# Two-layer GLA / short-convolution trunk on one core: TensorE order pinned in the ConvFFN, seven-product pairs for seven of eight convolution column tiles, split accumulation of the first two output products

## The chip, the cores and the metric

One core of a Trainium2 chip (trn2). The metric is the device time of one execution, in microseconds (us). Lower is better. The times are from the chip's own clock, the views from its hardware profiler.

## The reference, cut to what matters

Input x is (1, 512, 1024) in float32: 512 positions, model width 1024. Two layers, each a token mixer and a feed-forward, both with a residual:

```
layer 0: x += gla_mixer(rmsnorm(x));        x += conv_ffn(rmsnorm(x))
layer 1: x += short_conv_mixer(rmsnorm(x)); x += conv_ffn(rmsnorm(x))
out = rmsnorm(x)

conv_ffn(h):          up = causal_dwconv(h @ w_up, conv_w)     # 1024 -> 2 x 2816, 3 taps over positions
                      a, u = halves of up;  (silu(a) * u) @ w_down
short_conv_mixer(h):  b, c, u = thirds of h @ w_in             # 1024 -> 3 x 1024
                      (b * causal_dwconv(c * u, conv_w)) @ w_out
```

`causal_dwconv` is a depthwise convolution of width 3 over the positions.

## The kernel before, in words

**Layout.** Activations are held transposed: eight tiles `x[0..7]` of 128 channels x 512 positions. Every large product is made on TensorE in three terms: each operand is split into a high and a low part (`xh`, `xl` for activations, `wh`, `wl` for weights), and a product is wh*xh + wh*xl + wl*xh (`mm3`, line 302). A product group `group` (line 309) of eight 128-row blocks is therefore 24 matmuls of 512 columns; one of the FFN's down products, over a block of 6 or 5 gated tiles, is 18 or 15 of them.

**Seven products in place of eight.** Two column tiles of a projection that share the input (the `a` and `u` tiles of one FFN column, or the `c` and `u` tiles of one convolution column) can be made as a pair: seven half-size products (a Strassen form) in place of the eight that two groups amount to. `seven_first` (line 663) makes the first four, 48 matmuls of 256 columns, into two PSUM banks `updc` and `upab`; `seven_last` (line 680) the other three, 36 matmuls. The combinations are subtractions and additions of 256 columns on VectorE and copies on ScalarE (lines 670 to 689). The inputs they need beside `xparts`, sums and differences of x tiles named `t14..` and `t15..`, are made once per stage by `seven_sums` (line 598), called from `settle` (line 615) as the residual tiles come in, and split at the end of `settle`.

**Weights.** The class `Weights` (line 81) streams all weights in the order in which they are used. `load` starts a DMA on SyncE's queue into one of six raw buffers (`wr`, up to 512 KB each). `split_next` (line 163) makes a unit's `wh` on ScalarE (line 130) and its `wl` in one of two ways: on VectorE (line 135), or for units marked `added` by a negation on ScalarE (line 132) and an accumulating DMA issued from GpSimd (line 133). A pair takes two raw blocks and gives four units, q0 to q3 (`forms`, line 137): q0 needs two VectorE additions of the raw blocks (lines 144 and 146), the first into a buffer `s`, and q1 two more (150, 151); the halves are then split on ScalarE and VectorE. `take` (line 194) hands out the next unit and splits the one three further on. `wh` and `wl` have four buffers each.

**What sets the order.** The order of each engine's instructions is fixed when the kernel is compiled. A scheduler goes through a simulated clock: what stands earlier in the source goes first, but an instruction that is not ready by that clock gives way to a later one that is. On the chip each engine then keeps to the order so found, whether or not the data came when the simulated clock said. `tc.issue_after(ins)` puts what its block traces on the engine of `ins` behind `ins` in that order.

**The FFN** (`ffn_blocks`, line 692) goes through the list of `ff_steps` (line 213): column pairs 0 to 3 are made as plain groups ("up", "ua", "ub"), 4 to 21 by "s1" (`seven_first`) and "s2" (`seven_last`, then the convolution `conv` and `gate`). After each block of columns (`BLOCKS`, line 29) its eight down products "dn" are put between the steps of the next block. The steps around the end of the first block are, in the source:

```
... s1 5, ua 3, s2 5, s1 6, ub 3, s2 6, dn 0.0, s1 7, dn 0.1, s2 7, dn 0.2, s1 8, ...
```

`gate` makes the gated tile `g<j>` and splits it; `g3` (column 3, whose second half comes from "ub 3") is in `SOON`, that is, its low part is made on VectorE and not by the DMA.

**The convolution** (lines 744 to 769) makes columns 0, 1 and 7 as three plain groups `scc`, `scu`, `scb` and columns 2 to 6 (`SC_SEVEN`, line 32) as a pair around the group `scb`. Each column then goes through the three taps (`conv3`, line 362) and two multiplications, and is split into `s<i>`. The eight output products `so` follow as plain groups, each followed by `settle`. For the GLA's output products `go` (lines 638 to 643) the first two groups are already made together: blocks 0 to 5 of both, then blocks 6 and 7 of both.

Of the kernel before, what the change touches and what calls it, by code (L numbers as in the profile page):

```python
# [18 lines left out]
KD = D // P  # L19
# [9 lines left out]
BLOCKS = ((0, 6), (6, 11), (11, 16), (16, 22))  # L29
HALVED = 4  # L30
SOON = (3, 10, 15, 20, 21)
SC_SEVEN = (2, 3, 4, 5, 6)


@with_exitstack
def trunk_kernel(ctx, tc, xT, w_qk, w_v, w_g, w_up_gate, b_gate, w_go, w_sc, w_so, w_up, w_dn,
                 smalls, ff_cw, out):
    nc = tc.nc
    V, S, G, PE = nc.vector, nc.scalar, nc.gpsimd, nc.tensor
# [9 lines left out]
    def ps(name):  # L49
        return psp.tile([P, T], F32, tag="ps", name=name)  # L50
# [30 lines left out]
    class Weights:  # L81
# [3 lines left out]
        def __init__(self):  # L85
            self.units, self.srcs, self.need, self.last = [], [], [], []
            self.raw, self.split, self.hold = {}, {}, {}
            self.paired, self.added = set(), set()

            self.anchors = ()  # L90
            self.nl = self.ns = self.ng = 0

        def add(self, src, added=False):
# [43 lines left out]
        def forms(self, n, q, h, l):  # L137


            ra, rb = self.raw[n], self.raw[n + 1]  # L140
            lo, hi = slice(0, T), slice(T, 2 * T)
            if q == 0:
                s3 = bt(f"b13{'hl'[n % 4 // 2]}", f"s{n}")
                V.tensor_add(s3, ra[:, lo], rb[:, lo])  # L144
                self.halve(h[:, lo], l[:, lo], s3)
                V.tensor_add(rb[:, lo], rb[:, lo], rb[:, hi])
                self.halve(h[:, hi], l[:, hi], rb[:, lo])
            elif q == 1:
                self.halve(h, l, ra)
                V.tensor_add(ra[:, lo], ra[:, lo], rb[:, lo])  # L150
                V.tensor_add(ra[:, hi], ra[:, hi], ra[:, lo])
            elif q == 2:
                self.halve(h, l, rb[:, hi])
            else:
                self.halve(h, l, ra)
# [38 lines left out]
        def take(self):  # L194

            for _ in range(2):
                if self.nl < len(self.srcs) and (self.nl < 6 or self.last[self.nl - 6] < self.ns):
                    self.load()
                    if self.nl not in self.paired:
                        break  # L200
            self.part()
            self.ng += 1
            return self.split.pop(self.ng - 1)
# [9 lines left out]
    def ff_steps():  # L213
        steps = [("up", 0), ("up", 1), ("ua", 2), ("s1", 4), ("ub", 2), ("s2", 4), ("s1", 5), ("ua", 3), ("s2", 5)]

        middle = [("ub", 3)]
        for b in range(1, len(BLOCKS)):
            j0, j1 = BLOCKS[b]
            dn = [("dn", b - 1, m) for m in range(KD)]
            for j in range(j0, j1):  # L220
                steps += [("s1", j), middle.pop() if j == j0 else dn.pop(0), ("s2", j)]
                if j1 - j < len(dn) or j == j0 and b > 1:
                    steps.append(dn.pop(0))
            middle = dn
        return steps + middle + [("dn", len(BLOCKS) - 1, m) for m in range(KD)]
# [76 lines left out]
    def mm3(out, wparts, xparts, first, last, w_moving=False):  # L302
        (wh, wl), (xh, xl) = wparts, xparts
        terms = ((wh, xh), (wh, xl), (wl, xh)) if not w_moving else ((wh, xh), (wl, xh), (wh, xl))
        for i, (a, b) in enumerate(terms):
            a, b = (b, a) if w_moving else (a, b)
            PE.matmul(out, lhsT=a, rhs=b, start=first and i == 0, stop=last and i == 2)  # L307
# [325 lines left out]
    def residual(src, gi):  # L633
        for m in range(KD):
            settle(m, src(m), gi, True)


    go, w = [ps("go0"), ps("go1")], [take(), take()]
    for ks in (range(0, 6), range(6, 8)):
        for m in range(2):  # L640
            for k in ks:
                mm3(go[m], w[m][k], yparts[k], k == 0, k == KD - 1)
    residual(lambda m: go[m] if m < 2 else group(f"go{m}", yparts), 1)


    def product(out, ws, xs, first):
# [16 lines left out]
    def seven_first():  # L663

        dc, ab = ps("updc"), ps("upab")
        w1, w2 = halves(take())
        product(dc[:, lo], w1, tf[2], True)
        product(dc[:, hi], w2, tf[0], False)
        e = wk("e7", (P, HT), bufs=1)
        S.copy(e, dc[:, hi])  # L670
        V.tensor_sub(e, dc[:, lo], e)
        w1, w2 = halves(take())
        product(ab[:, lo], w1, cut(range(4), lo), True)
        product(ab[:, hi], w2, cut(range(4, 8), lo), False)
        u = wk("u", bufs=3)
        S.copy(u[:, lo], ab[:, hi])
        V.tensor_add(u[:, lo], u[:, lo], ab[:, lo])
        return dc, ab, e, u
# [11 lines left out]
        return u, u1  # L690

    def ffn_blocks(l, gnext):
        gp, cs, r = {}, {}, None

        def conv(j, i, u, src):
            V.tensor_mul(u, src, r)  # L696
            cs[j, i] = conv3(u, ffcw[:, l, i * NFF + j, :], f"c{i}", j == 0)

        def gate(j):
            a, u = cs.pop((j, 0)), cs.pop((j, 1))  # L700
            S.activation(a, a, AF.Silu)
            V.tensor_mul(u, u, a)
            gp[j] = split_to(u, f"g{j}", f"b{j % 11}", j not in SOON)

        for st in ff_steps():
            if st[0] == "dn":
                _, b, m = st
                last = b == len(BLOCKS) - 1
                if gnext is None and last and m == HALVED:
                    break  # L710
                part = group(f"dn{m}", [gp[j] for j in range(*BLOCKS[b])])
                if last and gnext is not None:
                    settle(m, part, gnext, False)
                else:
                    V.tensor_add(x[m], x[m], part)
                    if last:
                        norm_squares(m)
                continue
            step, j = st
            if step == "s1":  # L720
                begun = seven_first()
            elif step == "s2":
                for i, u in enumerate(seven_last(*begun)):
                    conv(j, i, u, u)
                gate(j)
            else:
                tiles = {"up": (0, 1), "ua": (0,), "ub": (1,)}[step]
                ups = {}
                for i in tiles:
                    ups[i] = group(f"up{i}", xparts)  # L730
                    if j == 0 and i == 0:
                        sums = sum_parts(acc[0])
                if j == 0:
                    r = inv_rms_rows(sums, D)
                for i in tiles:
                    conv(j, i, wk("u", bufs=3), ups[i])
                if 1 in tiles:
                    gate(j)
        return [gp[j] for j in range(*BLOCKS[-1])]

    ffn_blocks(0, 2)
# [3 lines left out]
    for i in range(KD):  # L745
# [20 lines left out]
        V.tensor_mul(cv, cv, r)  # L766
        V.tensor_mul(cv, cv, bp)
        yparts.append(split_to(cv, f"s{i}", f"b{i}", i < KD - 2))
    residual(lambda m: group(f"so{m}", yparts), 3)


    gp = ffn_blocks(1, None)
# [136 lines left out]
```

## Time and profile before

| | |
|---|---|
| median of 3 runs | 1097.52 us (1096.43 to 1100.97) |
| the profiled execution, its own time | 1096.32 us |
| its span, first to last instruction | 1094.6 us |
| mean granted TensorE clock | 0.994 of full speed |
| TensorE matmul busy | 1079.5 us (99%), 6502 matmuls |
| VectorE busy | 851.9 us (78%) |
| ScalarE busy | 684.2 us (63%) |
| DMA, mean over the span | 148 GB/s |

The profile is of one execution. Times in the views are microseconds from the start of the span. The FFN of layer 0 runs from about 211 to 561 us, the convolution from 561 to 689, its output products to 732.5, and the FFN of layer 1 from there to the end. PE is TensorE's matmuls, DVE VectorE, ACT ScalarE, POOL GpSimd, SP SyncE; L144 is line 144 of the kernel. In the timeline a bracket at the end of a row is the idle time of the engine ahead of the instruction and what ended it. Matmuls are pipelined: one row's duration overlaps the next, so the distance between starts is what counts.

### The profile page before, as it was taken

Reading aid. Unit: us, or ns where it says so; the run is one execution under the profiler, and the core shown is the slowest. Engines: PE = TensorE matmul, PEld = TensorE weight load, DVE = VectorE, ACT = ScalarE, POOL = GpSimd, SP = SyncE. Lnnn points to the kernel's source line nnn. Section 1 sums busy time; section 2 is a strip of 40 time slices with the busy share of each in tenths; the row PEclk is TensorE's granted clock in tenths of the full one; section 3 lists DMA queues with packets and bytes.
Section 4 is the critical chain, followed back from the end, with each engine's and each line's share of the span. In section 5 each row is a group of like instructions: output and inputs, shape, how many; then the busy total and the mean of one; then the engine's idle time right before and its main releaser. Section 6 shows DMA issues by size and latency. Waiting matters only on the chain.

```text
span 1094.6 us, 16998 instructions
## 1 busy us (share of the span) xinstructions
PE 1079.5 (99%) x6502; PEld 967.8 (88%) x6502; DVE 851.9 (78%) x1339; ACT 684.2 (63%) x1062; POOL 128.2 (12%) x160
## 2 busy tenths in 40 slices
PE   9999999999999999999999999999999999999997
PEld 7888888889899999999878998888989999999987
DVE  8874675789778989999678675477977888989954
ACT  7565765867656656666695455486755656666664
POOL 1000001101110111101111001011101011111120
PEclk9999999999999999999999999999999999999998
DMA  8332124865474564655897459386647556566573
GB/s 288 110 95 78 58 78 113 195 162 138 122 177 131 146 169 123 168 150 140 185 220 193 107 150 248 99 186 154 167 122 169 142 136 157 136 155 173 131 149 97
DMA packets 55958, 161.92 MB, mean 148 GB/s; under 512 B 6146, under 2 KB 8962, under 8 KB 55876
## 3 DMA queue, kind: packets, MB, share of 16 engines
q1 hardware_dynamic: 35428, 107.34, 31.1%
q0 software_dynamic: 20448, 53.49, 26.6%
q8 instruction: 51, 0.84, 0.3%
q14 instruction: 31, 0.25, 0.1%
HBM read 105.23 MB, written 2.10 MB: 98 GB/s over the span
## 4 chain that ended last, share of the span: by engine, by line
PE 68%; issue 3%; DMA 2%; DVE 1%; POOL 0%; ACT 0%; DVEq 0%; POOLq 0%; SPq 0%; ACTq 0%
PE updc L651 20%; PE dn L307 17%; PE upab L651 15%; PE scb L307 4%; PE so L307 4%; PE up L307 3%; PE dnl L307 2%; PE scu L307 1%; PE scc L307 1%; DMA wl<-wr 1%; DMA wr<-in_w_up 0%; POOL wl L133 0%; DVE wl L135 0%; DVE c L366 0%; DVE u L696 0%
## 5 line engine op out<-in xcount | busy, mean ns | idle before, releaser
L130 ACT CAST wh<-wr 128x1024 fp32r<-128x1024 f32 (+4 forms) x302 | 259.2, 863 | 187.3 <-PE upab L651 76.7
L135 DVE TENSOR_TENSOR wl<-wr,wh 128x512 fp32r<-128x512 f32 (+2 forms) x200 | 193.5, 981 | 60.0 <-ACT wh L130 59.2
L133 POOL DMA_DIRECT2D wl<-wr x102 | 89.2, 875 | 648.6 <-ACT wl L132 358.4
L365 ACT ACTIVATE c<-u,ffcw 128x512 f32<-128x512 f32 x88 | 59.3, 717 | 55.3 <-DVE u L696 55.3
L651 PE MATMUL upab<-xh,wh 128*128 128x256 f32 x328 | 92.8, 283 | 0.0
L651 PE MATMUL upab<-xl,wh 128*128 128x256 f32 x328 | 92.8, 283 | 0.0
L651 PE MATMUL upab<-xh,wl 128*128 128x256 f32 x328 | 92.8, 283 | 0.0
L132 ACT ACTIVATE wl<-wh 128x1024 fp32r<-128x1024 f32 (+2 forms) x102 | 90.8, 890 | 1.3
L366 DVE SCALAR_TENSOR_TENSOR c<-u,ffcw,c 128x511 f32<-128x511 f32 x88 | 62.4, 748 | 2.8 <-ACT c L365 2.6
L651 PEld LDWEIGHTS upab<-xh,wh 128*128 128x128 f32 x328 | 63.0, 192 | 0.0
L651 PEld LDWEIGHTS upab<-xl,wh 128*128 128x128 f32 x328 | 63.0, 192 | 0.0
L651 PEld LDWEIGHTS upab<-xh,wl 128*128 128x128 f32 x328 | 63.0, 192 | 0.0
L367 DVE SCALAR_TENSOR_TENSOR c<-u,ffcw,c 128x510 f32<-128x510 f32 x88 | 62.2, 746 | 0.0
L307 PE MATMUL up<-xh,wh 128*128 128x512 f32 x128 | 49.9, 390 | 0.0
L307 PE MATMUL up<-xl,wh 128*128 128x512 f32 x128 | 49.9, 390 | 0.0
L307 PE MATMUL up<-xh,wl 128*128 128x512 f32 x128 | 49.8, 389 | 0.0
L651 PE MATMUL updc<-xh,wh 128*128 128x256 f32 x164 | 46.4, 283 | 0.0
L651 PE MATMUL updc<-xl,wh 128*128 128x256 f32 x164 | 46.4, 283 | 0.0
L651 PE MATMUL updc<-xh,wl 128*128 128x256 f32 x164 | 46.4, 283 | 0.0
L696 DVE TENSOR_TENSOR u<-u,r 128x512 f32<-128x512 f32 x72 | 46.2, 684 | 0.0
L144 DVE TENSOR_TENSOR s<-wr,wr 128x512 f32<-128x512 f32 x41 | 28.2, 689 | 22.0 <-DMA wr<-in_w_up 15.3
L359 DVE RECIPROCAL r<-r 128x512 f32<-128x512 f32 x8 | 26.8, 3353 | 20.7 <-ACT r L358 20.7
(708 smaller groups left out, 3463.7 us busy)
## 6 DMA issues: line engine op xcount, KB each, us to landing
wr<-in_w_up SPq DMA_DIRECT2D x88, 512.0 KB, 3.9
wl<-wr POOLq DMA_DIRECT2D x38, 512.0 KB, 5.6
wr<-in_w_dn SPq DMA_DIRECT2D x32, 384.0 KB, 3.4
wl<-wr POOLq DMA_DIRECT2D x32, 384.0 KB, 4.1
wr<-in_w_sc SPq DMA_DIRECT2D x24, 512.0 KB, 4.4
wr<-in_w_dn SPq DMA_DIRECT2D x32, 320.0 KB, 3.2
wl<-wr POOLq DMA_DIRECT2D x32, 320.0 KB, 4.4
wr<-in_w_v SPq DMA_DIRECT2D x8, 512.0 KB, 3.7
```

What stands on the lines that cost most here:

```text
L130: S.copy(hh, src)
L132: S.activation(ll, hh.bitcast(F32), AF.Copy, scale=-1.0)
L133: G.dma_start(ll, src, accum_op=ALU.add)
L135: V.tensor_sub(ll, src, hh.bitcast(F32))
L144: V.tensor_add(s3, ra[:, lo], rb[:, lo])
L307: PE.matmul(out, lhsT=a, rhs=b, start=first and i == 0, stop=last and i == 2)
L359: V.reciprocal(r, r)
L365: a = S.activation(c, u, AF.Copy, scale=cw[:, 2:3])
L366: V.scalar_tensor_tensor(c[:, 1:], u[:, :T - 1], cw[:, 1:2], c[:, 1:], op0=ALU.mult, op1=ALU.add)
L367: v = V.scalar_tensor_tensor(c[:, 2:], u[:, :T - 2], cw[:, 0:1], c[:, 2:], op0=ALU.mult, op1=ALU.add)
L651: PE.matmul(out, lhsT=a, rhs=b, start=first and k == 0 and i == 0, stop=k == 3 and i == 2, skip_group_check=not first)
L696: V.tensor_mul(u, src, r)
```

## The change

Five edits. (1) `SC_SEVEN` is 1 to 7 in place of 2 to 6: convolution columns 1 and 7 are made as pairs as well. (2) The output products of the convolution are made as those of the GLA: the first two groups together, blocks 0 to 5 of both and then blocks 6 and 7 of both (`out_product`). (3) In the list of FFN steps the first down product of the first block moves behind the next "s1": `s2 6, s1 7, dn 0.0, s2 7, dn 0.1, s1 8, ...`; from column 10 on the list is as before. (4) In the FFN all TensorE instructions but those of the last eight down products are held to the order of the source (`manual_schedule`). (5) The two VectorE additions of a pair's unit q0 are queued behind the subtraction `e` (line 671) of the `seven_first` that was traced last, and the second of them moves ahead of the first split.

```diff
-SC_SEVEN = (2, 3, 4, 5, 6)
+SC_SEVEN = (1, 2, 3, 4, 5, 6, 7)
...
+            self.pace = None
...
             if q == 0:
                 s3 = bt(f"b13{'hl'[n % 4 // 2]}", f"s{n}")
-                V.tensor_add(s3, ra[:, lo], rb[:, lo])
+                with ExitStack() as behind:
+                    if self.pace is not None:
+                        behind.enter_context(tc.issue_after(self.pace))
+                    V.tensor_add(s3, ra[:, lo], rb[:, lo])
+                    V.tensor_add(rb[:, lo], rb[:, lo], rb[:, hi])
                 self.halve(h[:, lo], l[:, lo], s3)
-                V.tensor_add(rb[:, lo], rb[:, lo], rb[:, hi])
                 self.halve(h[:, hi], l[:, hi], rb[:, lo])
...
-                if j1 - j < len(dn) or j == j0 and b > 1:
+                if (j1 - j < len(dn) if j > j0 else b > 1):
                     steps.append(dn.pop(0))
...
-    go, w = [ps("go0"), ps("go1")], [take(), take()]
-    for ks in (range(0, 6), range(6, 8)):
-        for m in range(2):
-            for k in ks:
-                mm3(go[m], w[m][k], yparts[k], k == 0, k == KD - 1)
-    residual(lambda m: go[m] if m < 2 else group(f"go{m}", yparts), 1)
+    def out_product(name, gi):
+
+        o, w = [ps(f"{name}0"), ps(f"{name}1")], [take(), take()]
+        for ks in (range(0, 6), range(6, 8)):
+            for m in range(2):
+                for k in ks:
+                    mm3(o[m], w[m][k], yparts[k], k == 0, k == KD - 1)
+        residual(lambda m: o[m] if m < 2 else group(f"{name}{m}", yparts), gi)
+
+    out_product("go", 1)
...
-        V.tensor_sub(e, dc[:, lo], e)
+        W.pace = V.tensor_sub(e, dc[:, lo], e).ins
...
+        steps = ff_steps()
+        with tc.manual_schedule(engines={mybir.EngineType.PE}):
+            for st in steps[:-KD]:
+                take_step(st)
+        for st in steps[-KD:] if gnext is not None else steps[-KD:HALVED - KD]:
+            take_step(st)
         return [gp[j] for j in range(*BLOCKS[-1])]
...
-    residual(lambda m: group(f"so{m}", yparts), 3)
+    out_product("so", 3)
```

The body of the loop over the steps becomes the function `take_step`, otherwise unchanged.

## Rows read from the trace of the kernel before

**Rows 1.** The page's table of engines: busy time, share of the span, instructions.

```profile
PE 1079.5 (99%) x6502; PEld 967.8 (88%) x6502; DVE 851.9 (78%) x1339; ACT 684.2 (63%) x1062; POOL 128.2 (12%) x160
```

**Rows 2.** The table of waits: total us, times, longest; TensorE's largest entry.

```profile
PE dn L307 <- ACT g3h L130: 5.1, 2, 2.7
```

**Rows 3.** Timeline of TensorE, layer 0: start, duration, instruction, idle before.

```profile
284.92 0.40 PE L307 MATMUL dn<-g0h,wh 128*128 128x512 f32 x1
...
287.22 0.28 PE L651 MATMUL updc<-t150h,wl 128*128 128x256 f32 x1
290.21 0.70 PE L307 MATMUL dn<-g3h,wh 128*128 128x512 f32 x1 [2.71 <-ACT g3h L130]
...
299.33 0.40 PE L307 MATMUL dn<-g0h,wh 128*128 128x512 f32 x1
```

**Rows 4.** Timeline of TensorE, layer 1: the same two starts.

```profile
806.80 0.40 PE L307 MATMUL dn<-g0h,wh 128*128 128x512 f32 x1
...
821.10 0.40 PE L307 MATMUL dn<-g0h,wh 128*128 128x512 f32 x1
```

**Rows 5.** Chain of waits, an FFN stretch without idle time: start, length, work.

```profile
344.47 2.88 PE updc L651 x24
347.35 2.88 PE upab L651 x24
350.23 4.11 PE dn L307 x18
```

**Rows 6.** Busy time in windows; PEclk is the granted clock.

```profile
290.00:295.00 5.00, 4.79 (x18) 4.13 (x19) 5.00 (x10) 1.98 (x4) 0.00 (x0) 0.66 0.92 216
```

**Rows 7.** Timeline of VectorE, layer 0, ahead of that wait.

```profile
283.95 0.69 DVE L144 TENSOR_TENSOR s<-wr,wr 128x512 f32<-128x512 f32 x1 [4.24 <-issue]
284.56 0.68 DVE L696 TENSOR_TENSOR u<-up,r 128x512 f32<-128x512 f32 x1
...
290.68 0.69 DVE L135 TENSOR_TENSOR g3l<-c,g3h 128x512 fp32r<-128x512 f32 x1
```

**Rows 8.** Timeline of VectorE, layer 1, the same place.

```profile
805.52 0.69 DVE L144 TENSOR_TENSOR s<-wr,wr 128x512 f32<-128x512 f32 x1 [3.93 <-DMA wr<-in_w_up]
```

**Rows 9.** Chain of waits through the convolution and its output products.

```profile
578.82 5.44 PE scc L307 x24
...
595.14 2.87 PE updc L651 x24
...
610.67 2.88 PE updc L651 x24
...
626.21 2.88 PE updc L651 x24
...
689.18 43.52 PE so L307 x192
```

**Rows 10.** Timeline of TensorE and VectorE: end of column 6's pair, and its results.

```profile
672.55 0.28 PE L651 MATMUL upab<-t143h,wl 128*128 128x256 f32 x1
...
674.98 0.42 DVE L687 TENSOR_TENSOR u<-updc,u 128x256 f32<-128x256 f32 x1
...
683.62 0.69 DVE L135 TENSOR_TENSOR s6l<-c,s6h 128x512 fp32r<-128x512 f32 x1 [0.69 <-ACT s6h L130]
```

**Rows 11.** Busy time in windows: an FFN step, columns 6 and 7 (third value DVE).

```profile
423.43:436.93 13.50, 13.50 (x101) 12.89 (x100) 12.31 (x21) 8.45 (x14) 1.75 (x2) 1.00 0.43 121
...
657.13:672.67 15.54, 15.54 (x110) 14.58 (x109) 7.16 (x12) 9.98 (x13) 4.05 (x5) 1.00 1.04 249
672.67:689.02 16.35, 16.35 (x75) 13.53 (x73) 12.76 (x18) 5.36 (x7) 0.00 (x0) 1.00 0.65 206
```

**Rows 12.** Groups by line and shape: xcount | busy us, mean ns of one | idle before.

```profile
L135 DVE TENSOR_TENSOR wl<-wr,wh 128x1024 fp32r<-128x1024 f32 x112 | 136.7, 1222 | 56.4 <-ACT wh L130 56.1
```

**Rows 13.** Timeline of VectorE at the start of the convolution.

```profile
569.58 0.69 DVE L135 TENSOR_TENSOR t153l<-tl,t153h 128x512 fp32r<-128x512 f32 x1
...
575.83 3.35 DVE L359 RECIPROCAL r<-r 128x512 f32<-128x512 f32 x1 [4.87 <-ACT r L358]
```

**Rows 14.** Timeline of TensorE: the first group of the convolution.

```profile
562.20 0.50 PE L307 MATMUL scc<-xh,wl 128*128 128x512 f32 x1 [0.57 <-DMA wl<-wr]
```

More of the change, by code (lines that the diff above doesn't have):

```diff
@@ L692, in ffn_blocks @@
     def ffn_blocks(l, gnext):
-        gp, cs, r = {}, {}, None
+        gp, cs = {}, {}
+        r = sums = begun = None
         def conv(j, i, u, src):
@@ L703, in gate, with take_step @@
             gp[j] = split_to(u, f"g{j}", f"b{j % 11}", j not in SOON)
-        for st in ff_steps():
+        def take_step(st):
+            nonlocal r, sums, begun
             if st[0] == "dn":
@@ L708, in ffn_blocks @@
                 last = b == len(BLOCKS) - 1
-                if gnext is None and last and m == HALVED:
-                    break
                 part = group(f"dn{m}", [gp[j] for j in range(*BLOCKS[b])])
@@ L717, in ffn_blocks @@
                         norm_squares(m)
-                continue
+                return
             step, j = st
```

## The prediction

> **What bounds the kernel now.** I read the page's table of engines first: TensorE's matmuls are busy 99% of the span, every other engine 78% or less [rows 1]. Such a busy share alone does not say that TensorE works at its peak, so I then went down TensorE's timeline and looked at the distances between starts. From the output products of the GLA on they are those of a stream without holes: 43.52 us for 192 matmuls of 512 columns, 0.2267 us each [rows 9], and 2.88 us for 24 matmuls of 256 columns, 0.120 us each [rows 5]. The kernel is bound by TensorE's issue of matmuls. A change pays only where it takes matmuls out or closes a hole.
>
> The holes are few. In the table of waits TensorE's largest entry is one wait that occurs twice, 5.1 us in all: a down product waits for `g3h` [rows 2]. The timeline shows it in layer 0: dn 0.0 starts at 284.92 and goes through its first three blocks, three matmuls of "s1 7" follow, and then the array stands for 2.71 us until `g3h` is there [rows 3]. After it the granted clock is 0.66 in the mean over 290 to 295 us [rows 6]: part of that stretch ran at the lower of the two levels, 1.2 in place of 2.4 GHz, after TensorE had stood still. So the hole costs more than the wait. What it costs in all is read by comparing equal work: from the first matmul of dn 0.0 to that of dn 0.1 TensorE does one "dn" of 18 matmuls and one "s1" of 48. Without a hole these take 2.88 + 2.88 + 4.11 = 9.87 us [rows 5]. Here they took 299.33 - 284.92 = 14.41 [rows 3] in layer 0 and 821.10 - 806.80 = 14.30 [rows 4] in layer 1. **The loss is 4.54 and 4.43 us, 8.97 together.**
>
> Why `g3h` is late stands on VectorE. Its addition for the next pair's q0 (line 144) stands idle for 4.24 us before it starts [rows 7]; in layer 1 the same idle time, 3.93, is ended by the landing of a raw weight block [rows 8]. Behind that addition, in the same queue, sits the first operation on "ub 3", the multiplication `u<-up,r`, which starts at 284.56, the moment the addition is over; `g3l` ends 6.81 us after that, at 291.37 [rows 7]. The addition was put there by the compiler, whose simulated clock took the block to be landed.
>
> **The change part by part.** *The moved step (edit 3).* With "s1 7" ahead of dn 0.0, the product starts not at 284.92 but 5.76 us later, at 290.68, and asks for `g3h` after its first three blocks, 9 x 0.2267 = 2.04 us on, at 292.7. In the old trace `g3h` was there at 290.2 [rows 3] and `g3l` at 291.37 [rows 7]. So even if VectorE still stood for the raw block, both are there, by 1.3 us or more. What "s1 7" needs, its weights q0 and q1, sits ahead in the stream either way; q0 is now split one unit earlier in the source. Late next would be q1, which "s1 7" needs 2.88 us after its start.
>
> *The additions behind `e` (edit 5).* Unit q0 of a pair is split during the step before, after that step's `seven_first`. Its two additions now wait in VectorE's queue behind `e`, after that step's first 24 matmuls, 2.88 us [rows 5], and a copy on ScalarE, some 3.5 us in. Behind them on VectorE wait the split of q0 and whatever the scheduler puts later; TensorE waits for q0 at the next "s1". The tightest step is 13.50 us long with VectorE busy for 12.31 of it [rows 11], so about 10 us remain for two additions of 0.69 and two half splits of 0.69 [rows 7]. Cost on the path: nothing, covered by those 10 us; without that cover, each us late is a us of TensorE. The gain is that the multiplication on "ub 3" is no longer held up by the raw block, some 4 us more margin for `g3`. Edits 3 and 5 cure the same hole, so together they bring its 8.97 us once. Bounds: 0 (another operand is late at the new place) and 8.97. I take 8.97, since two margins stand behind it.
>
> *The fixed order (edit 4).* In the old trace the order on TensorE differs from that of the source only at these two places; everywhere else in both FFNs "s1", "dn" and "s2" come as listed. So it removes the three stray matmuls of rows 3 and moves nothing else: 0. It does take away the compiler's filling in.
>
> *Two more pairs (edit 1).* A column of three plain groups takes 595.14 - 578.82 = 16.32 us, one with a pair 626.21 - 610.67 = 15.54 [rows 9], so each pair saves 0.78, **1.56 for two**. The Trainium skill (TensorE: Matmul & The Clock Gate, Back-to-back issue gap) gives a warm gap of N/2.4 + 2.5 ns, that is 216 ns for 512 columns and 109 for 256; by it 48 x 216 - 84 x 109 would save 1.2 us per pair, 2.4 in all. The rows say 0.2267 and 0.120 us, and I go by the rows. What a pair adds elsewhere: on VectorE four additions and three half splits of 0.69 [rows 7], two whole splits of 1.22 [rows 12] and five operations of 0.42 [rows 10], 9.4 us; on GpSimd two accumulating DMAs fewer; on SyncE the same loads in the same order. For column 1 this starts in VectorE's idle 4.87 us ahead of the reciprocal, and the `t` tiles, which are now wanted at 578.8 and no longer at 595.1 [rows 9], are written by 570.3 [rows 13]. For column 7 VectorE has 7.16 + 12.76 us busy of the last 31.9 [rows 11]; with 9.4 more it is full but not over. I cost that at nothing on the path up to the output products.
>
> *The output products (edit 2).* They save no matmul. They are the cover for column 7, whose three taps now start only when its last product is done. From the end of column 6's pair (672.55 + 0.28) to the end of `s6l` (683.62 + 0.69) it was 11.5 us [rows 10], with about 2.4 us of weight splits in between (two of 1.22 [rows 12]), so 9.1 to 11.5 us. The cover is 36 matmuls (blocks 0 to 5 of two groups), 8.16 us, and block 6 of the first group, 0.68; the low part of `s7` is wanted one matmul later, at 9.07. The hole is 0 to 2.4 us. The scheduler may also pull block 6 of the second group ahead, 0.68. I take 0.7. The first two `settle` calls move together, later by 4 us for the first one only; the last one, which the next FFN waits for, stays.
>
> Sum: -8.97 - 1.56 + 0.7 = -9.8 us. On the profiled execution's 1096.32 that is 1086.5; the median of the runs shown, 1097.52, lies 1.2 above it and would give 1087.7. I say **1087.0**. Ends from the costs alone: without the hole of column 7 and without the 0.57 us that the first group waits [rows 14], 1084.5; with its full 2.4 us, 1088.2, on the upper base 1089.4.
>
> **The rivals.** *A: a new hole around the convolution's pairs.* Column 7's chain or the first pair's weights come 2 to 3 us late, and the clock falls as it did after the wait of 2.71 us, which cost 4.54. For it: VectorE is full there. Against: the five pairs of before flow without a hole, one every 15.54 us [rows 9]. It gives back about 4.5: 1087.0 + 4 = 1091.
>
> *B: the FFN's hole is only moved.* "s1 7" or dn 0.0 now waits for a split weight, which VectorE had behind the raw block. Half of the 8.97 stays: 1091.5. Against: q0 and q1 move earlier along with everything VectorE does.
>
> *C: slower.* The additions behind `e` make q0 late in every step, because VectorE is 91% busy [rows 11] and its order was laid out by a simulated clock; with the order fixed, TensorE cannot do a later product meanwhile. There are 17 such hand-overs per FFN, 34 in all (columns 5 to 21). The gain of 9.8 is gone at 0.29 us per step, and by 0.6 us each the time is 1097 + 20 - 10 = 1107. Against: the 10 us of room.
>
> *D: nothing.* The hole stays, because `g3` is as late by the new schedule as its consumer: 1096.
>
> **How the numbers follow.** The forecast has 0.62, A 0.14, B 0.10, D 0.06, C 0.08. The range 1084 to 1093 holds the forecast, and A and B but for their upper ends, about 0.83. A measurement here tells about 0.5%, 5.5 us, from no change: faster means under 1092.0, slower over 1103.0. Faster: 0.62, most of A and half or more of B, 0.77. Same: the rest of A and B, D and the milder part of C, 0.15. Slower 0.08.
>
> **What would show it.** Right: in the table of waits TensorE's wait for `g3h` is gone, from the start of dn 0.0 to the start of "s2 7" it takes 4.1 us, no window in either FFN has a granted clock under 1.00, and `s` (line 144) comes after `e` on VectorE. Columns 1 and 7 take 15.5 us each. At the first `so` groups a hole of under 1.5 us. Wrong: TensorE waiting for `wl` at "s1" all through the FFNs (C), for `s7` by 2 us with the clock down after it (A), or for anything around 285 to 293 us (B, D).

## The result, and the profile after

| | before | changed |
|---|---|---|
| median of 4 runs each | 1097.3 us (1096.43 to 1100.97) | 1086.14 us (1085.82 to 1086.49) |
| ratio, 95% interval | | 0.9892 (0.9869 to 0.9915) |
| profiled execution, its own time | 1096.32 us | 1086.49 us |
| its span, mean granted clock | 1094.6 us, 0.994 | 1084.8 us, 0.997 |

The changed kernel is 1.1% faster. The forecast was 1087.0, 0.9 above the median. The two profiled spans lie 1094.6 - 1084.8 = 9.8 us apart, the size of the forecast's sum.

Where the 9.8 us came from is read on TensorE's timeline: the starts of the first matmuls of each stage, subtracted from one another. For later use the table has the two kernels of the experiments that have the cleanest convolution with five and with seven pairs.

| stage of TensorE | before | changed | five pairs, no hole | seven pairs, no hole |
|---|---|---|---|---|
| start to the GLA's output products | 167.14 | 167.65 | 167.09 | 166.92 |
| first FFN, first `up` to first `scc` | 350.36 | 345.78 | 345.76 | 345.81 |
| convolution, to the first `so` | 128.00 | 126.24 | 127.14 | 125.55 |
| its output products, to the next `up` | 43.52 | 43.92 | 43.52 | 43.91 |
| second FFN, to the first `dnl` | 333.92 | 329.49 | 329.46 | 329.96 |

(five pairs: `e4_five_pairs`, seven: `g4_dve_splits`, both below.) The FFNs became 4.58 and 4.43 us shorter, 9.01 in all; the convolution 1.76; its output products 0.40 longer; the start 0.5 longer, which varies by as much from one execution to another (166.88 to 167.65 over all profiles here).

The page's table of engines, changed kernel; it answers to [rows 1]. There are 72 matmuls more and 4.7 us less of busy time.

```profile
PE 1074.8 (99%) x6574; PEld 967.2 (89%) x6574; DVE 871.6 (80%) x1367; ACT 684.4 (63%) x1070; POOL 124.4 (11%) x156
```

The table of waits, changed kernel, TensorE's four largest entries (total us, times, longest). The entry for `g3h` of [rows 2] is gone. What is largest now lies at the kernel's first and last matmuls; the fourth is the convolution's first group, as in [rows 14].

```profile
PE warm L76 <- DVE warm L64: 1.5, 1, 1.5
PE sums L811 <- DVE sq L802: 0.6, 1, 0.6
PE rb L824 <- DVE rl L818: 0.6, 1, 0.6
PE scc L313 <- DMA wl<-wr: 0.4, 1, 0.4
```

TensorE's timeline, changed kernel, at the place of [rows 3] and [rows 4] (start, duration, instruction). From the first matmul of dn 0.0 to the first of "s2 7" it takes 295.31 - 291.20 = 4.11 us in layer 0 and 811.24 - 807.14 = 4.10 in layer 1, the 4.11 of a `dn` without a hole in [rows 5].

```profile
291.20 0.40 PE L313 MATMUL dn<-g0h,wh 128*128 128x512 f32 x1
...
295.31 0.28 PE L660 MATMUL updc<-t150h,wh 128*128 128x256 f32 x1
...
807.14 0.40 PE L313 MATMUL dn<-g0h,wh 128*128 128x512 f32 x1
...
811.24 0.28 PE L660 MATMUL updc<-t150h,wh 128*128 128x256 f32 x1
```

Busy time in windows, changed kernel (the value after POOL's is the granted clock): the stretch of [rows 6], and column 7 as a pair. The first has a clock of 1.00 in place of 0.66, and TensorE busy throughout; so have all 138 windows of 5 us over the two FFNs, 211 to 556 us and 727 to 1072. In the second VectorE has 11.17 of 15.54 us.

```profile
290.00:295.00 5.00, 5.00 (x29) 4.35 (x28) 5.00 (x10) 2.77 (x7) 0.86 (x1) 1.00 0.75 213
...
667.65:683.19 15.54, 15.54 (x110) 14.58 (x109) 11.17 (x16) 6.14 (x9) 0.66 (x1) 1.00 0.75 208
```

VectorE's timeline, changed kernel, layer 0, at the place of [rows 7]. The multiplication `u<-up,r` starts at 281.98, where it was 284.56, and `g3l` at 287.75 in place of 290.68, though everything starts 0.5 us later here. The pair's addition `s` stands behind `e`, at 294.01, and has no idle time.

```profile
281.98 0.68 DVE L706 TENSOR_TENSOR u<-up,r 128x512 f32<-128x512 f32 x1
...
287.75 0.69 DVE L137 TENSOR_TENSOR g3l<-c,g3h 128x512 fp32r<-128x512 f32 x1
...
290.68 0.42 DVE L680 TENSOR_TENSOR e<-updc,e 128x256 f32<-128x256 f32 x1
...
294.01 0.68 DVE L149 TENSOR_TENSOR s<-wr,wr 128x512 f32<-128x512 f32 x1
```

The chain of waits, changed kernel, through the convolution, as in [rows 9]: column 1's `c` and `u` products begin at 574.58 and the next column's at 590.11, 15.53 us later; column 7's begin at 667.81 and the output products at 683.35, 15.54 later. The output products take 43.92 us to 727.27.

```profile
574.58 2.87 PE updc L660 x24
...
590.11 2.88 PE updc L660 x24
...
667.81 2.88 PE updc L660 x24
...
683.35 9.32 PE so L313 x41
...
727.27 10.88 PE up L313 x48
```

### The profile page after: what moved, and what is told of

Same layout as the page of the kernel before. It is cut to its first block, busy times and chain, and to the rows that moved or that the text cites. A ratio compares the mean times of both kernels' runs of the same rounds, so it can differ in the third digit from the quotient of the medians.

```text
span 1084.8 us, 17188 instructions
## 1 busy us (share of the span) xinstructions
PE 1074.8 (99%) x6574; PEld 967.2 (89%) x6574; DVE 871.6 (80%) x1367; ACT 684.4 (63%) x1070; POOL 124.4 (11%) x156
## 4 chain that ended last, share of the span: by engine, by line
PE 95%; issue 2%; DMA 1%; POOL 0%; DVE 0%; SPq 0%; ACT 0%; DVEq 0%; POOLq 0%
PE updc L660 23%; PE dn L313 17%; PE upab L660 17%; PE up L313 8%; PE so L313 4%; PE scb L313 4%; PE g L313 4%; PE v L313 4%; PE go L313 4%; PE k L313 2%; PE q L313 2%; PE dnl L313 2%; DMA wl<-wr 1%; PE o L536 1%; PE scu L313 1%
## 5 line engine op out<-in xcount | busy, mean ns | idle before, releaser
L137 DVE TENSOR_TENSOR wl<-wr,wh 128x1024 fp32r<-128x1024 f32 (+2 forms) x208 | 200.6, 980 | 56.5 <-ACT wh L132 56.0
L135 POOL DMA_DIRECT2D wl<-wr x98 | 84.8, 865 | 657.8 <-ACT wl L134 316.2
L660 PE MATMUL upab<-xl,wh 128*128 128x256 f32 x344 | 97.4, 283 | 0.0
L660 PE MATMUL upab<-xh,wl 128*128 128x256 f32 x344 | 97.4, 283 | 0.0
L660 PE MATMUL upab<-xh,wh 128*128 128x256 f32 x344 | 97.4, 283 | 0.0
L134 ACT ACTIVATE wl<-wh 128x1024 fp32r<-128x1024 f32 (+2 forms) x98 | 86.5, 883 | 1.4
L660 PEld LDWEIGHTS upab<-xh,wl 128*128 128x128 f32 x344 | 66.1, 192 | 0.0
L660 PEld LDWEIGHTS upab<-xh,wh 128*128 128x128 f32 x344 | 66.1, 192 | 0.0
L711 ACT ACTIVATE c<-c 128x512 f32<-128x512 f32 x44 | 27.8, 632 | 31.7 <-DVE c L373 31.5
L724 DVE TENSOR_TENSOR x<-x,dn 128x512 f32<-128x512 f32 x52 | 35.7, 686 | 13.0 <-PE dn L313 12.0
```

The lines of the kernel that those rows point to most:

```text
L134: S.activation(ll, hh.bitcast(F32), AF.Copy, scale=-1.0)
L135: G.dma_start(ll, src, accum_op=ALU.add)
L137: V.tensor_sub(ll, src, hh.bitcast(F32))
L660: PE.matmul(out, lhsT=a, rhs=b, start=first and k == 0 and i == 0, stop=k == 3 and i == 2, skip_group_check=not first)
```

## The experiments

Twelve kernels ran, in three groups of four; each group has its own runs of the kernel before, on its own chip. Medians and ratios go against those. "Hole" means idle time of TensorE.

**One part alone: which edit closes the FFN's hole?** The kernel before in this group: 1097.51 us (1094.43 to 1099.03, 13 runs).

`e1_step`: the kernel before with edit 3 alone.

```diff
-                if j1 - j < len(dn) or j == j0 and b > 1:
+                if (j1 - j < len(dn) if j > j0 else b > 1):
```

> The kernel before with edit 3 alone (dn 0.0 behind s1 7). Theory (two margins, either of edits 3 and 5 enough): the wait for g3h is gone, dn 0.0 to s2 7 takes 4.1 us in both layers, and the time falls by the whole hole, 8.97 us, to about 1088.3. On VectorE the addition for the next pair still stands ahead of the multiplication on ub 3 and may still idle, without cost. Rival (the hole is only moved, B of the prediction): TensorE waits for something else near 285 to 293 us and less than 6 us are gained.

Measured: 1086.37 us (1086.21 to 1086.93), ratio 0.9902 (0.9884 to 0.9921); the FFNs take 345.76 and 329.42. The moved step alone closes the hole. (The median lies 2 us under the 1088.3 expected: it falls by 11.1 us, more than the hole of the one profiled execution; the point on the sum below comes back to this.) VectorE's timeline of this kernel, layer 0, shows that it does so in a way that the forecast did not have: the addition `s` is still ahead of the multiplication, but it no longer stands idle, and `g3l` starts at 287.07.

```profile
280.18 0.69 DVE L144 TENSOR_TENSOR s<-wr,wr 128x512 f32<-128x512 f32 x1
280.78 0.69 DVE L696 TENSOR_TENSOR u<-up,r 128x512 f32<-128x512 f32 x1
...
287.07 0.68 DVE L135 TENSOR_TENSOR g3l<-c,g3h 128x512 fp32r<-128x512 f32 x1
```

The raw block was there sooner. SyncE's timeline of the kernel before shows the loads in the order of the list of steps: dn 0.0, the two of "s1 7", dn 0.1 and dn 0.2, the two of "s1 8". The addition that stood idle belongs to the last two, the pair of column 8. From the start of the first of these to the end of the second it takes 7.57 us:

```profile
256.54 0.33 SPq L124 DMA_DIRECT2D wr<-in_w_dn  x1
256.96 1.08 SPq L124 DMA_DIRECT2D wr<-in_w_up  x2
266.63 6.24 SPq L124 DMA_DIRECT2D wr<-in_w_dn  x2
272.96 7.57 SPq L124 DMA_DIRECT2D wr<-in_w_up  x2
```

and in `e1_step`, where the list is "s1 7", dn 0.0, dn 0.1, "s1 8", the same two take 1.78:

```profile
256.58 0.80 SPq L124 DMA_DIRECT2D wr<-in_w_up  x2
257.49 9.30 SPq L124 DMA_DIRECT2D wr<-in_w_dn  x2
272.37 1.78 SPq L124 DMA_DIRECT2D wr<-in_w_up  x2
```

The waits of SyncE's queue in the kernel before, between those two loads (273.36 to 280.2 us), name what held the second, an accumulating DMA:

```profile
SPq L124 <- DMA wl<-wr: 6.8, 1, 6.8
```

The semaphores of the loads in the trace say which buffer it was: the second load of "s1 8" waits for the load at 256.54, dn 0.0's block, and for the accumulating DMA issued at 274.55, which reads that block. In `e1_step` the two loads of "s1 8" take buffers of earlier `in_w_up` loads (242.33 and 239.71), and the one that waits for dn 0.0's DMA is the next, a down block at 286.37, where it holds up no addition.

`e2_pace`: the kernel before with edit 5 alone.

```diff
-                V.tensor_add(s3, ra[:, lo], rb[:, lo])
+                with ExitStack() as behind:
+                    if self.pace is not None:
+                        behind.enter_context(tc.issue_after(self.pace))
+                    V.tensor_add(s3, ra[:, lo], rb[:, lo])
+                    V.tensor_add(rb[:, lo], rb[:, lo], rb[:, hi])
                 self.halve(h[:, lo], l[:, lo], s3)
-                V.tensor_add(rb[:, lo], rb[:, lo], rb[:, hi])
...
-        V.tensor_sub(e, dc[:, lo], e)
+        W.pace = V.tensor_sub(e, dc[:, lo], e).ins
```

> The kernel before with edit 5 alone (additions of q0 behind e), dn 0.0 in its old place. Theory: g3h is ready some 3 to 4 us earlier, which nearly closes the hole: a wait of 0.5 to 1 us per layer at dn 0.0 remains, the clock does not fall, and 6 to 8 us of the 8.97 are gained, 1089 to 1091. Rival (C of the prediction in small): the later additions make q0 late at the steps, TensorE waits for wl in updc, and the gain is under 4 us.

Measured: 1086.88 us (1086.68 to 1087.22), ratio 0.9907 (0.9888 to 0.9925); the FFNs take 345.92 and 329.62. It brings nearly all of the gain too, where a hole of 0.5 to 1 us was to stay. TensorE's timeline, layer 0: dn 0.0 is still ahead of "s1 7", three strays fill in, and `g3h` and `g3l` are used without a wait worth the name.

```profile
286.95 0.39 PE L311 MATMUL dn<-g3h,wh 128*128 128x512 f32 x1
...
287.57 0.50 PE L311 MATMUL dn<-g3l,wh 128*128 128x512 f32 x1
```

SyncE's load is held as long as ever, now harmlessly, since the addition that needs it comes behind `e`, at 295.04, and has no idle time:

```profile
273.69 8.16 SPq L125 DMA_DIRECT2D wr<-in_w_up  x2
```

So edits 3 and 5 cure one hole by different means: the first brings the block sooner, the second takes the multiplication out from behind it.

`e3_order`: the kernel before with edit 4 alone.

```diff
-        for st in ff_steps():
+        steps = ff_steps()
+        with tc.manual_schedule(engines={mybir.EngineType.PE}):
+            for st in steps[:-KD]:
+                take_step(st)
+        for st in steps[-KD:] if gnext is not None else steps[-KD:HALVED - KD]:
+            take_step(st)
```

> The kernel before with edit 4 alone (TensorE held to source order in the FFN); the order differs from before only in the 8 updc matmuls that stood inside dn 0.0. Theory: the hole at g3h stays and opens earlier and wider, 3.2 us of wait in place of 2.7 and 2.4, with the clock down after it; the time is 0 to 2 us longer than before, 1097 to 1099. Rival: pinning the order moves other engines enough to close the hole, under 1092.

Measured: 1100.23 us (1095.32 to 1104.87, 10 runs), ratio 1.002 (1.0007 to 1.0033): slower than before, by 2.7 us in the medians where 0 to 2 were expected (0.8 to 3.6 by the ratio's interval). The stray matmuls no longer fill in. In the profiled execution, the slowest of the ten, VectorE's addition stood idle longer than in [rows 7], 6.85 us,

```profile
286.51 0.69 DVE L146 TENSOR_TENSOR s<-wr,wr 128x512 f32<-128x512 f32 x1 [6.85 <-DMA wr<-in_w_up]
```

and TensorE waited 5.66 us for `g3h` here and 4.5 in layer 1 (total, times, longest):

```profile
PE dn L310 <- ACT g3h L132: 10.2, 2, 5.7
```

Each FFN takes 9.1 to 9.2 us more than without a hole (354.98 and 338.55). The edit that fixes the order costs something by itself; beside the moved step it changes nothing in TensorE's order (`g3_step_pairs_out`, below).

`e4_five_pairs`: the changed kernel with the pairs of before.

```diff
-SC_SEVEN = (1, 2, 3, 4, 5, 6, 7)
+SC_SEVEN = (2, 3, 4, 5, 6)
```

> The changed kernel with five pairs in the convolution again (columns 1 and 7 as plain groups). Theory: each of the two columns takes 16.3 us in place of 15.5, and the small hole at s7 (0.3 us) goes; the time is 1.2 to 1.6 us above the changed kernel's 1086.14, 1087.3 to 1087.7. Rival: the pairs' extra VectorE work costs elsewhere, so that five pairs are as fast as seven, within 0.4 us.

Measured: 1086.42 us (1086.35 to 1087.01), ratio 0.9903 (0.9885 to 0.9921). The median misses the 1087.3 to 1087.7 expected and lies 0.3 us above the changed kernel's 1086.14, within the 0.4 of the rival. By the stages the pairs are worth 127.14 - 125.55 = 1.59 us in the convolution and lose 43.91 - 43.52 = 0.39 at the output products: 1.2. By the ratios it is 0.0011, about 1.2 us, against the changed kernel's first comparison, but 0.0006, 0.7 us, against the repetition below (both well inside the intervals). The size is read from the stages; the medians alone don't settle it.

**The changed kernel taken apart.** The kernel before in this group: 1097.33 us (1096.21 to 1099.37, 7 runs).

`f1_changed_again`: the changed kernel once more, no edit.

> The changed kernel once more, unaltered, so that the next three can be compared with it under the same conditions. Expected: 1085.8 to 1086.5 us. The hole of 0.66 us at the first group of the convolution, which waits for an accumulating DMA, is there in some profiled executions and not in others; if it is a matter of the DMA's luck, it may be gone here, and if the pair of column 1 causes it, it is there again.

Measured: 1086.10 us (1085.57 to 1086.25), ratio 0.9897 (0.9883 to 0.9912). The convolution takes 125.75 us, and its first group has no wait this time: that wait belongs to an execution, not to column 1's pair.

`f2_so_in_turn`: edit 2 undone for the convolution.

```diff
-    out_product("so", 3)
+    residual(lambda m: group(f"so{m}", yparts), 3)
```

> The changed kernel with edit 2 undone: the output products of the convolution one after the other. Theory now: the compiler fills in by itself, TensorE's order differs in the place of three matmuls only (block 6 of the first or second group), so the time is within 0.4 us of the changed kernel. Rival (the prediction's reason for the edit, a cover for column 7): without it TensorE waits 3 to 4 us for s7, the clock falls, and the time is 4 us or more longer.

Measured: 1086.33 us (1085.55 to 1087.65), ratio 0.9902 (0.9887 to 0.9916). The output products take 43.89 us, as with the edit. The two orders on TensorE differ in three matmuls: where the source takes the groups in turn, the compiler itself puts the second group's blocks ahead of the first group's `s7`. Edit 2 is worth nothing here. The profiled execution is the slowest of its four and shows something else, a hole at column 4's `b` products, ended by an accumulating DMA; the convolution takes 127.84 us in it (what made that DMA late stands in the last section):

```profile
628.39 0.50 PE L313 MATMUL scb<-xh,wl 128*128 128x512 f32 x1 [2.01 <-DMA wl<-wr]
```

`f3_six_pairs`: column 7 as plain groups again.

```diff
-SC_SEVEN = (1, 2, 3, 4, 5, 6, 7)
+SC_SEVEN = (1, 2, 3, 4, 5, 6)
```

> The changed kernel with column 7 as plain groups, column 1 still a pair. Theory: column 7 is 0.78 us longer and the 0.4 us at the first output products go, so the time is 0.2 to 0.5 us above the changed kernel. Rival: column 7's pair costs more than it saves (its hole varies with the execution), and six pairs are as fast or faster.

Measured: 1086.50 us (1085.76 to 1086.93), ratio 0.9901 (0.9886 to 0.9916). The convolution takes 126.66 us and the output products 43.52 again, without a hole: the 0.4 us there belongs to column 7's pair.

`f4_dn_early`: edit 3 undone, 4 and 5 kept.

```diff
-                if (j1 - j < len(dn) if j > j0 else b > 1):
+                if j1 - j < len(dn) or j == j0 and b > 1:
```

> The changed kernel with edit 3 undone: dn 0.0 ahead of s1 7 as before, with the order of TensorE fixed and the additions of q0 behind e. Theory: edit 5 alone frees the multiplication on ub 3, g3h comes within 0.6 us of when dn 0.0 asks for it, the clock stays up, and the time is 0.3 to 1.5 us above the changed kernel. Rival: with nothing to fill in, the wait is long enough to take the clock down, and 4 us or more are lost.

Measured: 1086.61 us (1086.16 to 1086.94), ratio 0.9903 (0.9887 to 0.992). With edit 5 there, edit 3 is worth some 0.5 us by the medians. By the stages it is 0.5 in each layer, 10.39 us from dn 0.0 to dn 0.1 in place of 9.87, at one wait of 0.23 us each; in layer 0:

```profile
287.61 0.50 PE L313 MATMUL dn<-g3l,wh 128*128 128x512 f32 x1 [0.23 <-DVE g3l L137]
```

**Is there a margin behind the moved step?** The kernel before in this group: 1096.28 us (1094.32 to 1097.95, 7 runs). In both of the next kernels the multiplication on "ub 3" is made three times with the same result, so that `g3` is late on purpose.

`g1_late_behind`: this in the changed kernel.

```diff
-            V.tensor_mul(u, src, r)
+            for _ in range(3 if (j, i) == (3, 1) else 1):
+                V.tensor_mul(u, src, r)
```

> The changed kernel with the multiplication on ub 3 (column 3, second half) made three times over on VectorE, the same result each time, so that g3 comes about as late as in the kernel before (g3l some 2.5 to 3 us later, near 291). Theory (the moved step alone covers the old lateness): dn 0.0 asks for g3h at 293, so there is no hole and the time stays within 0.5 us of 1086.1. Rival: the 5.76 us are used up by other work and a hole of over 1 us per layer opens.

Measured: 1085.34 us (1085.22 to 1085.36), ratio 0.9898 (0.9883 to 0.9913): nothing lost. `g3l` starts at 289.02, 1.3 us later than in the changed kernel though this execution's FFN began 0.8 us sooner, so the delay is some 2 us, less than intended.

`g2_late_early`: the same delay, with edit 3 undone (its diff is that of `f4_dn_early` and that of `g1_late_behind`).

> The same delay, and edit 3 undone: dn 0.0 ahead of s1 7, additions of q0 behind e, order fixed. Theory: with dn 0.0 early nothing covers the delay; TensorE waits 2 to 3 us for g3h in each layer, more than the wait is lost if the clock falls, and the time is 4 to 10 us above 1086.1. Rival: under 2 us, if the lateness of g3 did not set the hole.

Measured: 1091.92 us (1090.74 to 1092.64), ratio 0.9957 (0.9942 to 0.9973), 6.6 us over `g1_late_behind` and 5.3 over `f4_dn_early` of the group above, which is this kernel without the delay. The waits are shorter than the 2 to 3 us expected. TensorE's timeline, both layers:

```profile
288.94 0.49 PE L313 MATMUL dn<-g3h,wh 128*128 128x512 f32 x1 [1.57 <-ACT g3h L132]
...
806.57 0.49 PE L313 MATMUL dn<-g3h,wh 128*128 128x512 f32 x1 [1.57 <-ACT g3h L132]
```

The same wait of 1.57 us, with one of 0.25 for `g3l` behind it in both layers, made the work from dn 0.0 to dn 0.1 take 12.25 us in layer 0 and 13.79 in layer 1; against 9.87 that is 2.4 and 3.9 us. (The second FFN as a whole is 4.6 longer than without a hole, 334.10 - 329.5; the other 0.7 lies at a wait of 0.41 us for an accumulating DMA at 960.96, the place that `g4_dve_splits` below shows too.) The windows behind the two waits differ in the granted clock, 1.00 and 0.69:

```profile
290.00:295.00 5.00, 5.00 (x37) 4.68 (x36) 4.81 (x9) 3.45 (x5) 0.00 (x0) 1.00 0.43 108
...
808.00:813.00 5.00, 5.00 (x26) 4.38 (x25) 4.77 (x8) 2.81 (x4) 0.00 (x0) 0.69 0.35 90
```

So the moved step has a margin of its own, as the forecast had it: about 2 us of delay cost nothing behind it and over 5 ahead of it.

`g3_step_pairs_out`: edits 1, 2 and 3 alone; edits 4 and 5 undone.

```diff
-                with ExitStack() as behind:
-                    if self.pace is not None:
-                        behind.enter_context(tc.issue_after(self.pace))
-                    V.tensor_add(s3, ra[:, lo], rb[:, lo])
-                    V.tensor_add(rb[:, lo], rb[:, lo], rb[:, hi])
+                V.tensor_add(s3, ra[:, lo], rb[:, lo])
                 self.halve(h[:, lo], l[:, lo], s3)
+                V.tensor_add(rb[:, lo], rb[:, lo], rb[:, hi])
...
-        W.pace = V.tensor_sub(e, dc[:, lo], e).ins
+        V.tensor_sub(e, dc[:, lo], e)
...
-        with tc.manual_schedule(engines={mybir.EngineType.PE}):
-            for st in steps[:-KD]:
-                take_step(st)
+        for st in steps[:-KD]:
+            take_step(st)
```

> The changed kernel with edits 4 and 5 undone (order not fixed, additions of q0 free): edits 1 to 3 remain. TensorE's order is the changed kernel's, instruction by instruction. Theory: the moved step is enough, the time is within 0.4 us of 1086.1. Rival: the additions of q0, free to stand early in VectorE's queue, block it at some steps again, a hole of over 1 us opens somewhere in the FFNs.

Measured: 1087.05 us (1086.92 to 1087.22), ratio 0.9914 (0.9899 to 0.9929), 1.7 above `g1_late_behind`, more than expected. It is not the FFNs: they take 345.81 and 329.50, and TensorE's order is the changed kernel's to the last matmul, though nothing fixes it. In its profile the convolution takes 126.94 us, 1.4 over the seven pairs without a hole, with two waits for accumulating DMAs (total, times, longest):

```profile
PE scc L310 <- DMA wl<-wr: 0.5, 1, 0.5
...
PE scb L310 <- DMA wl<-wr: 0.3, 1, 0.3
```

That accounts for this execution; that the other three had the same waits is not shown, though all four lie within 0.3 us of one another. The rival's blocked additions are there too, in the convolution and not in the FFNs: the waits of VectorE from 556 to 684 us have

```profile
DVE s L146 <- DMA wr<-in_w_sc: 8.2, 5, 3.8
```

where the two profiles of the changed kernel have no such wait. At the first group they can't be the cause, since it comes before them. At the `b` products, column 3's, they may be: an addition stands idle for 1.69 us until 598.41, the taps, ScalarE and the issue of the DMA at 605.87 (604.08 in the changed kernel) follow it, and TensorE waits at 612.08. So edit 5 may be worth something in the convolution with seven pairs, which no run here tests by itself.

`g4_dve_splits`: the changed kernel, with the low parts of the pairs' `b` weights and of column 0's `c` made by VectorE, not by ScalarE and an accumulating DMA.

```diff
-            W.add(b, True)
+            W.add(b)
...
-                W.add(src, True)
+                W.add(src, src is not c)
```

> A version that the runs point to: the changed kernel with the low parts of the seven weights b of the pairs in the convolution, and of c of column 0, made on VectorE and no longer by an accumulating DMA. Theory: the holes at scb of column 4 and at the first scc, which wait for that DMA in some executions (0 to 2.2 us), go; VectorE, busy for 11 to 13 of 15.5 us per column, takes 1.22 us more. The time is 0.3 to 1 us below the changed kernel's, 1085.1 to 1085.8. Rival: VectorE is then late with the pairs' splits and the time is the same or longer.

Measured: 1085.52 us (1085.47 to 1086.74), ratio 0.9903 (0.9886 to 0.9921). The convolution has no hole, 125.55 us. The second FFN has a small wait for an accumulating DMA, in the last down product of the second block:

```profile
PE dn L313 <- DMA wl<-wr: 0.2, 1, 0.2
```

The same place costs 0.2 to 0.3 us in `f1_changed_again` and `g1_late_behind` too (read from the starts), so it is not the price of this edit; in the first profile of the changed kernel it costs nothing. The kernel ties with `g1_late_behind`, which has the changed kernel's splits, at 1085.34. No version among these is measurably better than the changed kernel.

## Why the prediction was right, point by point

**What bounds the kernel, and the hole term.** Forecast: 4.54 + 4.43 = 8.97 us. Measured in the stages: 4.58 + 4.43 = 9.01. Comparing equal work with and without the hole gave the whole loss, wait and clock together, and it came back in whole. "Together they bring its 8.97 us once" is shown by `e1_step`, `e2_pace` and `f4_dn_early`: either of edits 3 and 5 is enough.

**The moved step.** The forecast argued by a margin, with VectorE perhaps still standing for the raw block. The margin is there (`g1_late_behind` against `g2_late_early`). But it was not needed: the stall itself went, because moving the step also moved the raw blocks in SyncE's queue. The forecast asked whether the weights of "s1 7" are "ahead in the stream either way". They are, but the addition that stood belongs to the pair of column 8, and the forecast did not ask which buffer its load waits for: that of dn 0.0. That is a step with a right sum and an incomplete cause.

**The additions behind `e`.** Cost forecast as nothing, measured as nothing: `f4_dn_early`, with edits 4 and 5, has FFNs of 346.30 and 330.14 us, 0.5 and 0.65 over the changed kernel's 345.78 and 329.49, and 0.5 of each lies at dn 0.0, where the wait is for `g3l`; the changed kernel's hold the two additions behind `e` and have no hole. Rival C, which needs a wait for `wl` at every step, is not seen in any profile.

**The fixed order.** Forecast as 0, and the loss of the compiler's filling in named. Both hold (though by TensorE's timeline eight matmuls of "s1 7" stood inside dn 0.0, three ahead of the wait and five behind it, where the forecast counts three): `g3_step_pairs_out` has the same order on TensorE without it, and `e3_order` shows what the filling in was worth where a hole is left.

**The pairs.** Forecast 0.78 each, 1.56. The stages without a hole give 127.14 - 125.55 = 1.59. By an estimate from the warm gap that the Trainium skill states (TensorE: Matmul & The Clock Gate, Back-to-back issue gap) it would be 2.4 us for the two; the trace does not bear that out, the rows' spacings do. The forecast's 9.4 us of VectorE for a pair came out as (871.6 - 851.9) / 2 = 9.85. In the two profiled executions the difference was 1.76, since the first group's hole, weight wait and what came with it, was 0.87 us long in one (128.00 - 127.13) and 0.69 in the other (126.24 - 125.55).

**The output products.** Forecast +0.7, measured +0.40. The estimate of 9.1 to 11.5 us for column 7's chain holds: from the end of column 7's products at 683.35 it is 10.0 us to the end of `s7l` at 692.66 + 0.69, VectorE's timeline of the changed kernel, and TensorE wants it at 693.48,

```profile
692.66 0.69 DVE L137 TENSOR_TENSOR s7l<-c,s7h 128x512 fp32r<-128x512 f32 x1 [0.69 <-ACT s7h L132]
```

so the cover is 0.4 us short, most of it already at `s7h`. Wrong was whose cover it is: the forecast gave it to edit 2, and `f2_so_in_turn` has it without. The forecast named the compiler's pulling ahead for one block and did not ask whether it would do the rest as well.

**The sum and its base.** -9.8 forecast on the profiled execution, -9.8 measured on it. That the two agree so closely is in part luck: the stages that were changed make -9.01 - 1.76 + 0.40 = -10.37, and the start, longer by 0.51 in this execution, takes the rest back. The forecast's low end has a slip: without column 7's hole and the first group's 0.57 the costs give 1086.5 - 0.7 - 0.57 = 1085.2, and 1084.5 takes the 0.7 off twice. Against the medians the gain is 11.2: the kernel before varies from 1094.4 to 1099.0 over 13 runs and the changed kernel from 1085.6 to 1086.5 over eight, and the profiled execution of before, at 1096.32, lies below its median. That the hole is the source of that spread fits `e3_order`, where it was longer and the runs spread over 9.6 us. The granted clock on record for each run goes the same way: of the 27 runs of the kernel before beside the experiments, the two at 0.996 took 1094.3 and 1094.4 us, the 14 at 0.994 took 1097.2 in the mean, and the five at 0.992 and 0.993 took 1098.3 to 1099.4. Where in those runs the clock fell is not shown. The forecast took 1087.0 between the two bases, 0.9 too high.

**The rivals.** B and D are out: TensorE has no wait between 285 and 300 us, nor at the same place of layer 1. A came in a small form that the forecast did not have: waits of 0 to 2 us, ended by an accumulating DMA, at `scc` or `scb`, in some executions and not in others, and the clock stayed up after them. In the profiles that show them they eat part of what the two pairs bring: over the profiles with seven pairs the convolution takes 125.5 to 127.8 us, against 127.13 to 127.14 in the four kernels with five pairs beside the one before.

## What to carry to other kernels

Price a hole by equal work with and without it, from start to start, not by the wait alone: here 2.7 us of waiting were 4.5 us of time, and the whole came back. When an operation in an in-order queue waits for a load, follow it one step further, to the buffer that the load itself waits for, and to what still reads that buffer: changing the order in which buffers are asked for and moving the operation out of the way each cured it alone. Before crediting an edit with a cover, ask what the compiler's own order does without it.

## What the runs showed of the hardware

**One wait, two prices.** The same 1.57 us of idle TensorE, and 0.25 behind it, cost 2.4 us where the granted clock stayed at 1.00 (2.4 GHz) and 3.9 us where it fell to 0.69 in the mean of 808 to 813 us, part of them at 1.2 GHz; both are in one execution of `g2_late_early`, at the same place of the two layers. The wait of 2.01 us in `f2_so_in_turn` was not followed by a fall; those of 5.66 and 4.5 us in `e3_order` were, and with those for `g3l` behind them they cost 9.2 and 8.5 us (19.05 and 18.40 from dn 0.0 to dn 0.1, against 9.87). The windows behind the first of them have:

```profile
293.00:298.00 5.00, 4.57 (x12) 3.29 (x13) 5.00 (x10) 1.96 (x3) 0.00 (x0) 0.50 0.86 216
295.00:300.00 5.00, 5.00 (x23) 4.41 (x22) 5.00 (x8) 2.28 (x3) 0.00 (x0) 0.61 0.45 143
```

What decides between the two outcomes after a short wait stays open.

**Weights come late in two ways.** With the same program on TensorE, the convolution of the changed kernel had no listed wait for an accumulating DMA in one profile (`f1_changed_again`) and 0.40 us in the other, and 2.01 in a kernel that differs from it in three matmuls. The median from issue to landing of these 512 KB transfers is 5.3 us in both profiles of the changed kernel. At the first group it is the single transfer that is slow: issued at 549.54 in the changed kernel, waited for until 557.97, 8.4 us; it is 8.6 in the kernel before and in `g3_step_pairs_out`. These are the three profiles with that wait. Why is not shown.

```profile
549.54 0.87 POOL L135 DMA_DIRECT2D wl<-wr  x1 [3.90 <-ACT wl L134]
```

The longest wait, in `f2_so_in_turn`, is another matter. There the DMA was issued at 622.37, in `f1_changed_again` at 620.20, and TensorE had it 6.0 us later. Late was a plain load of raw weights before it, issued at 607.56 and used from 613.91 on, 6.35 us later; in `f1_changed_again` it was 607.44 and 611.75, 4.31 us. ScalarE, whose queue also makes the part that the accumulating DMA adds to, stood for that load (ScalarE's timelines, `f1_changed_again` first):

```profile
611.75 0.62 ACT L132 CAST wh<-wr 128x512 fp32r<-128x512 f32 x1 [4.04 <-DMA wr<-in_w_sc]
...
613.91 0.62 ACT L132 CAST wh<-wr 128x512 fp32r<-128x512 f32 x1 [5.95 <-DMA wr<-in_w_sc]
```

So a wait that an accumulating DMA ends may have begun at a load that delayed the engine ahead of it.
